# One layer of a hybrid encoder on one core: the input projection as 7 block products, done whole before the branches

## The chip, the cores and the metric

The kernel runs on one core of a Trainium2 chip. The metric is the device time of one execution in microseconds, the median of several runs. The profiler also records one execution of its own.

## The reference, cut to what matters

544 token rows (512 of a new stream, 32 of a running one) of width 2048 go through one layer. All of it is float32.

```python
mod = jax.nn.silu(c) @ w_ada + b_ada                 # shift, scale, gate: one vector per stream
h = rmsnorm(x, norm_g) * (1.0 + scale) + shift       # 544 x 2048
z = h @ w_in                                         # 2048 x 15360, split into ten parts
ya = gmlp_mix(gelu(au), rmsnorm(gelu(av))) * silu(ag)            # gMLP branch, 1024 wide
yb = rglru(causal_conv(lx)) * silu(lg)                           # RG-LRU branch, 1024 wide
yc = rmsnorm(hgrn2_scan(silu(hq), hf, hi)) * silu(hg)            # HGRN2 branch, 8 heads of 128
ga, gb, gc = split(sigmoid(mg), 3)                               # mg: 3 x 2048 columns of z
out = (ga * (ya @ w_a) + gb * (yb @ w_b) + gc * (yc @ w_c)) @ w_out
y = rmsnorm(x + gate * out, final_g)
```

z has 120 column blocks of 128: 8 each for au, av, ag, lx, lg, hq, hf, hi, hg and 48 for mg.

## The kernel before, in words

Activations lie transposed: 128 features on the partitions, 544 tokens along the free axis, in two halves of 272 (`HF`). The products run in float32r, and every operand is split in two parts, `wh` (rounded) and `wl` (the rest), so that one float32 product becomes three matmuls: `wh`·high, `wh`·low, `wl`·high (line 213). A weight piece of 128 x 1024 is loaded by SyncE's queue into `raw` (line 1171), copied by ScalarE into `wh` (through the helper `act`, line 154) and subtracted by VectorE into `wl` (line 1189). This is `prepare`; it runs two items ahead (`AHEAD`), and `wh` and `wl` have three buffers each.

The work is a list of items, written in the order in which they run. An item is one weight piece: 8 row blocks x 3 matmuls x 2 halves = 48 matmuls of 272 columns. A column block of z (`z_block`) is two items, a block of a branch product (`p_block`) one, a block of the out product (`o_block`) two. For each item the loop issues loads, then the item's `pre`, then `prepare(i + 2)`, then its matmuls, then its `post`, which empties the accumulator `pm`; then `pump()` lets every running generator do one step up to its next `yield`. The generators hold the rest of the branches: `av_gen` and `gm_gen` (gMLP), `hg_gen` (13 steps for each HGRN2 head), `lru_gen`, `gate_gen` (the gate vector of `mod`, line 1043, on VectorE), `yc_gen`, `mix_gen`. Each engine takes its instructions in the order in which they were issued.

The order of the stages is: the start (64 items of `w_ss` for shift and scale, line 367; under them the first three column blocks of z, lines 402 to 421); gMLP; HGRN2, four column blocks of z to a head; the merge of branch 0 (for each of 16 output blocks a column block of mg, then a `p_block`); the merge of branch 2; RG-LRU; the merge of branch 1; the out product. So column blocks of z are spread over all stages but the last. Everything between the stages stays in on-chip memory (`arena_t`, 26 pieces of 552 columns).

Of the kernel before, what the change touches and what calls it, by code (L numbers as in the profile page):

```python
# [7 lines left out]
F32 = mybir.dt.float32  # L8
# [5 lines left out]
NP = 512  # L14
# [26 lines left out]
SLOT = T + 8  # L41
SMALL = 256


class Arena:


    def __init__(self, t, slots, smalls):
        self.t = t
        self.slots, self.smalls = slots, smalls  # L50
        self.busy = [False] * slots
        self.small_busy = [False] * smalls
        self.at = self.small_at = 0

    def get(self, n):
        if n <= SMALL:
            order = [(self.small_at + i) % self.smalls for i in range(self.smalls)]
            k = next((i for i in order if not self.small_busy[i]), None)
            if k is None:
                raise MemoryError("no small piece left")  # L60
            self.small_busy[k] = True
            self.small_at = (k + 1) % self.smalls
            o = self.slots * SLOT + k * SMALL
            return self.t[:, o:o + n], ("s", k, 1)
        m = -(-n // SLOT)
        if m == 1:
            order = [(self.at + i) % self.slots for i in range(self.slots)]
        else:
            order = range(self.slots - m, -1, -1)
        k = next((i for i in order if not any(self.busy[i:i + m])), None)  # L70
        if k is None:
            raise MemoryError(f"no {m} slots in a row: {self.busy}")
        for i in range(k, k + m):
            self.busy[i] = True
        if m == 1:
            self.at = (k + 1) % self.slots
        return self.t[:, k * SLOT:k * SLOT + n], ("b", k, m)

# [3 lines left out]
    def free(self, r):  # L82
        kind, k, m = r
        busy = self.small_busy if kind == "s" else self.busy
        for i in range(k, k + m):
            busy[i] = False


class Buf:
    def __init__(self, arena, n):  # L90
        self.arena, self.n = arena, n
        self.ap, self.r = arena.get(n)
        self.col = self.r[1] * SLOT

# [11 lines left out]
def hybrid_step_kernel(ctx: ExitStack, tc: tile.TileContext, xT, cT, w_first, w_in, w_branch, w_out,  # L106
# [4 lines left out]
    const = ctx.enter_context(tc.tile_pool(name="const", bufs=1))  # L111
    wp = ctx.enter_context(tc.tile_pool(name="wp", bufs=3))
    ps = ctx.enter_context(tc.tile_pool(name="ps", bufs=2, space=PSUM))

    h_a = const.tile([128, KW, 2, T], F32R, name="h_a")
    h_b = {}
    yH = const.tile([128, KW, 2, T], F32R, name="yH")
# [4 lines left out]
    masks = const.tile([128, len(LEVELS), 2, 128], U8, name="masks")  # L122
# [9 lines left out]
    cs = const.tile([128, KD, 2], F32, name="cs")  # L132
    outs_conv = const.tile([128, KW, 2, 3], F32, name="outs_conv")
    outs_h = const.tile([128, KW, 2], F32, name="outs_h")
    NSLOT, NSMALL = 26, 5
    arena_t = const.tile([128, NSLOT * SLOT + NSMALL * SMALL], F32, name="arena_t")
    arena = Arena(arena_t, NSLOT, NSMALL)

    def buf(n=T):
        return Buf(arena, n)  # L140
# [26 lines left out]
    def pm():  # L167
        return ps.tile([128, 2, 512], F32, tag="m", name="pm", bufs=2)
# [19 lines left out]
    def hT(k):  # L188
        return h_a[:, k] if k < KW else h_b["t"][:, k - KW]

    def yT_in(k):
        return yH[:, k]

    def split(dst, src):
        act(dst[:, 0, :], src, AF.Copy)
        tt(dst[:, 1, :], src, dst[:, 0, :].bitcast(F32), op=OP.subtract)


    items = []

    def item(src, width, mul, post=None, pre=None, plain=False):
        items.append((src, width, mul, post, pre, plain))

    def group_item(src, kt, rhs, acc, first, last, post, pre=None, hs=(0, 1)):
# [1094 lines left out]
```

## Time and profile before

| | us |
|---|---|
| median of 3 runs (2178.68 to 2179.18) | 2178.73 |
| the profiled execution, its own time | 2176.01 |
| its span, first to last instruction | 2174.3 |
| TensorE (PE) busy in the span | 2128.7 |
| VectorE (DVE) busy | 891.0 |
| ScalarE (ACT) busy | 761.2 |
| GpSimd (POOL) busy | 287.9 |

Matmuls are pipelined, so that the busy time of PE is the time in which at least one is under way; PEld is the load of the stationary operand. The span is what the rows below divide up; the time of an execution lies 1.7 us above it, and the median of the runs 2.7 us above that.

### The profile page before, as it was taken

The numbers are of one execution on the slowest core, as the hardware profiler recorded it, in microseconds if no ns is written. First come the engines' busy times: TensorE is split into PE (matmuls) and PEld (weight loads), VectorE is DVE, ScalarE is ACT, GpSimd is POOL, SyncE is SP. The second block draws the span as 40 slices with busy tenths as digits, with TensorE's granted clock in tenths as the row PEclk, the third lists the DMA queues.
The fourth block names the chain that finished last, engine by engine and source line by source line (L and its number), as shares of the span: only waits on it lengthen the run. The fifth ranks groups of instructions, "written<-read, shape, count | busy, mean of one in ns | idle before, by whom it ended". The sixth has DMA issues, their size and how long they took to land.

```text
span 2174.3 us, 39091 instructions
## 1 busy us (share of the span) xinstructions
PE 2128.7 (98%) x17048; PEld 2070.3 (95%) x17048; DVE 891.0 (41%) x1306; ACT 761.2 (35%) x1116; POOL 287.9 (13%) x308
## 2 busy tenths in 40 slices
PE   6989999999999999999999999999999999999997
PEld 3689999999999999999999999999999999999997
DVE  3432323344444444222223655525555352244225
ACT  3233433455455555322222222224655222233223
POOL 0000100212233333000000010011111001111112
PEclk9999999999999999999999999999999999999999
DMA  9942222222222222222222544422222442223334
GB/s 354 392 137 85 83 86 79 89 70 73 82 75 70 80 73 72 82 84 89 90 87 82 169 142 144 127 81 82 90 86 90 128 136 89 88 86 122 106 123 146
DMA packets 77355, 241.95 MB, mean 111 GB/s; under 512 B 8608, under 2 KB 15040, under 8 KB 77184
## 3 DMA queue, kind: packets, MB, share of 16 engines
q1 hardware_dynamic: 75184, 236.96, 33.4%
q8 instruction: 134, 2.20, 0.4%
q10 hardware_dynamic: 1376, 1.28, 0.2%
q0 software_dynamic: 624, 1.21, 0.2%
q14 instruction: 37, 0.30, 0.0%
HBM read 233.75 MB, written 5.67 MB: 110 GB/s over the span
## 4 chain that ended last, share of the span: by engine, by line
PE 94%; DMA 2%; DVE 1%; ACT 1%; issue 0%; SPq 0%; POOL 0%; DVEq 0%; ACTq 0%
PE pm L213 86%; DMA arena_t<-in_w_first_dram 1%; PE px L651 1%; PE pm L421 1%; ACT arena_t L154 1%; PE px L367 1%; PE po L304 0%; PE po L421 0%; PE px L730 0%; DMA raw<-in_w_in_dram 0%; PE px L511 0%; PE po L787 0%; PE px L770 0%; DMA arena_t<-in_xT_dram 0%; PE px L653 0%
## 5 line engine op out<-in xcount | busy, mean ns | idle before, releaser
L213 PE MATMUL pm<-h_b,wh 128*128 128x272 f32 x4256 | 714.4, 289 | 0.0
L213 PE MATMUL pm<-h_a,wh 128*128 128x272 f32 x4256 | 712.8, 289 | 0.1
L1189 DVE TENSOR_TENSOR wl<-raw,wh 128x1024 fp32r<-128x1024 f32 (+1 forms) x328 | 404.8, 1234 | 604.4 <-ACT wh L154 601.3
L213 PEld LDWEIGHTS pm<-h_a,wh 128*128 128x128 f32 x4256 | 603.1, 188 | 1.8 <-ACT wh L154 0.3
L213 PEld LDWEIGHTS pm<-h_b,wh 128*128 128x128 f32 x4256 | 601.4, 188 | 1.9 <-ACT wh L154 1.4
L154 ACT ACTIVATE wh<-raw 128x1024 fp32r<-128x1024 f32 (+1 forms) x328 | 339.1, 1037 | 522.7 <-PE pm L213 474.4
L213 PE MATMUL pm<-h_a,wl 128*128 128x272 f32 x2128 | 443.1, 288 | 0.8 <-DVE wl L1189 0.8
L213 PE MATMUL pm<-h_b,wl 128*128 128x272 f32 x2128 | 443.6, 288 | 0.0
L213 PEld LDWEIGHTS pm<-h_b,wl 128*128 128x128 f32 x2128 | 336.4, 188 | 0.0
L213 PEld LDWEIGHTS pm<-h_a,wl 128*128 128x128 f32 x2128 | 334.5, 188 | 1.0 <-DVE wl L1189 1.0
L213 PE MATMUL pm<-yH,wh 128*128 128x272 f32 x1536 | 255.5, 288 | 0.0
L154 ACT ACTIVATE arena_t<-pm 128x544 f32<-128x544 f32 (+3 forms) x143 | 80.2, 573 | 440.4 <-PE pm L213 431.6
L213 PEld LDWEIGHTS pm<-yH,wh 128*128 128x128 f32 x1536 | 217.4, 188 | 0.2
L1006 POOL TENSOR_TENSOR arena_t<-arena_t 128x544 f32<-128x544 f32 x32 | 61.0, 1906 | 793.4 <-DVE arena_t L1004 739.7
L213 PE MATMUL pm<-yH,wl 128*128 128x272 f32 x768 | 158.5, 288 | 0.0
L154 ACT ACTIVATE arena_t<-arena_t 128x272 f32<-128x272 f32 (+6 forms) x181 | 98.5, 583 | 160.0 <-DVE arena_t L1101 100.3
L213 PEld LDWEIGHTS pm<-yH,wl 128*128 128x128 f32 x768 | 120.2, 188 | 0.0
L1043 DVE SCALAR_TENSOR_TENSOR arena_t<-arena_t,cs 128x512 f32<-128x512 f32 x120 | 92.1, 826 | 10.2 <-DMA arena_t<-in_w_gate_dram 10.2
L1004 DVE TENSOR_TENSOR arena_t<-pm,arena_t 128x544 f32<-128x544 f32 x48 | 34.8, 725 | 146.7 <-PE pm L213 146.7
L154 ACT ACT_TABLE_LOAD x59 | 75.7, 1283 | 30.7 <-PE pm L213 25.2
L154 ACT ACTIVATE arena_t<-px 128x512 f32<-128x512 f32 (+3 forms) x96 | 34.6, 377 | 84.9 <-PE px L754 32.2
L154 ACT ACTIVATE yH<-arena_t 128x544 fp32r<-128x544 f32 (+1 forms) x40 | 27.2, 693 | 96.9 <-DVE arena_t L915 36.9
(218 smaller groups left out, 1220.2 us busy)
## 6 DMA issues: line engine op xcount, KB each, us to landing
raw<-in_w_in_dram SPq DMA_DIRECT2D x234, 512.0 KB, 3.7
raw<-in_w_ss_dram SPq DMA_DIRECT2D x54, 512.0 KB, 9.8
raw<-in_w_branch_dram SPq DMA_DIRECT2D x48, 512.0 KB, 3.5
raw<-in_w_out_dram SPq DMA_DIRECT2D x38, 512.0 KB, 3.8
arena_t<-in_w_gate_dram SPq DMA_DIRECT2D x64, 256.0 KB, 4.2
arena_t<-in_xT_dram SPq DMA_DIRECT2D x16, 544.0 KB, 6.7
arena_t<-in_w_ss_dram SPq DMA_DIRECT2D x10, 512.0 KB, 7.0
out_yT_dram<-arena_t SPq DMA_DIRECT2D x12, 272.0 KB, 2.6
```

Source lines behind the costliest of these rows:

```text
L154: return nc.scalar.activation(out, in_, func, **kw)
L213: mm(p[:, h, :HF], w[:, s], rhs(k)[:, r, h * HF:(h + 1) * HF], start=first and i == 0 and q == 0, stop=last and i == n - 1 and q == 2)
L367: mm(p[32 * i:32 * i + 32, part * 256:part * 256 + 256], cz[:, 4 * q + i, :], w[:, i * 256:(i + 1) * 256], start=q == 0, stop=q == 3)
L421: mm(firsts[g][:, h, :HF], w[:, s], hT(k)[:, r, h * HF:(h + 1) * HF], start=k == 0 and q == 0, stop=k == KD - 1 and q == 2)
L651: mm(fv(p, 64 * i, [[128, 2], [1, 64]]), x[:, 256 * i + 128:256 * i + 256], fv(x, 256 * i, [[256 + m, 2], [2 * m, nb], [1, m]]), start=Tru ...
L1004: tt(two(g.ap), halves(p), two(g.ap), op=OP.mult)
L1006: ptt(mix[j].ap, mix[j].ap, g.ap, op=OP.add)
L1043: stt(acc[s].ap, b.ap, c, acc[s].ap, op0=OP.mult, op1=OP.add)
L1189: tt(wl[:, :width], t[:, :width], wh[:, :width].bitcast(F32), op=OP.subtract)
```

## The change

h is cut into 2 x 2 blocks (two halves of the tokens, two halves of the 2048 features), and a pair of column blocks of z with its 2048 weight rows into 2 x 2 blocks as well. One level of Strassen's scheme (in Winograd's form) makes the four block products of the pair's outputs out of 7 products instead of 8: `group`. A product is an item of 8 x 3 = 24 matmuls of 272 columns. The seven sums of h (`X[1]` to `X[7]`) are formed once, in the start (`sums`); the weight sums are formed for every pair on VectorE, into the raw pieces and one buffer `t2`; VectorE adds up the outputs in `after`. There are 60 pairs, all done in one stretch directly after the start (`z_groups`). The three column blocks that ran under the start now run there too.

There isn't room on the chip for z, so blocks go to device memory: hf, hq, hi, hg and all of mg by `keep`, av after its gelu, and the finished branch outputs ya and yb. gMLP and RG-LRU run as generators under the pairs; the gates of RG-LRU are plain float32 matmuls now (4 for a block, before 12 in float32r). Then `merges` runs the three branches' products, 16 `p_block`s each, with no column blocks of z between them: branch 0 with HGRN2 heads 0 to 3, branch 1 with heads 4 to 7 and `gate_gen`, and branch 2 after the last head. A `p_block` lets the generators step three times (after 18, 36 and 48 matmuls). The gate blocks of mg, the partial sums `mix`, ya, yb and a head's four blocks are loaded from device memory on GpSimd's queue, which also takes the loads of `gate_gen` and, in the out product, of x.

```diff
+PRODUCTS = (1, 6, 2, 5, 7, 3, 4)
+RAWS = 6
+    def halved(src, width=1024):
+        wh = wp.tile([128, 1024], F32R, tag="wh", name="wh", bufs=3)
+        wl = wp.tile([128, 1024], F32R, tag="wl", name="wl", bufs=3)
+        split(wh[:, :width], wl[:, :width], src[:, :width])
+        return wh, wl
+    def rows3(p, w, rhs, kt, start, stop, **kw):
+        wh, wl = w
+        n = len(kt)
+        for i, k in enumerate(kt):
+            s = slice(i * 128, (i + 1) * 128)
+            for q, (a, r) in enumerate(((wh, 0), (wh, 1), (wl, 0))):
+                mm(p, a[:, s], rhs(k, r), start=start and i == 0 and q == 0,
+                   stop=stop and i == n - 1 and q == 2, **kw)
+    def group(b1, b2, post, posts=None):
...
+                if i == 1:
+                    g["w", 1] = halved(raws[n11])
+                elif i == 6:
+                    a, b, c = raws[n11], raws[n12], raws[n22]
+                    tt(a, b, a, op=OP.subtract)
+                    t = g["t"] = late["t2"]
+                    tt(t, c, a, op=OP.subtract)
+                    g["w", 6] = halved(t)
+                elif i == 2:
+                    g["w", 2] = halved(raws[n21])
+                elif i == 5:
+                    g["w", 5] = halved(raws[n11])
+                    done[n11] = True
+                elif i == 7:
+                    tt(raws[n12], raws[n22], raws[n12], op=OP.subtract)
+                    g["w", 7] = halved(raws[n12])
+                    done[n12] = True
+                elif i == 3:
+                    g["w", 3] = halved(raws[n22])
+                    done[n22] = True
+                elif i == 4:
+                    t = g["t"]
+                    tt(t, raws[n21], t, op=OP.subtract)
+                    g["w", 4] = halved(t)
+                    done[n21] = True
...
+        bank = {1: 0, 2: 0, 6: 1, 5: 2, 3: 2, 7: 3, 4: 3}
...
+                if i == 1:
+                    g["u"] = buf(HF)
+                    act(g["u"].ap, b, AF.Copy)
+                elif i == 6:
+                    tt(g["u"].ap, b, g["u"].ap, op=OP.add)
+                elif i == 2:
+                    g["o1"] = buf()
+                    act(g["o1"].ap[:, :HF], b, AF.Copy)
+                elif i == 5:
+                    g["o2"] = buf()
+                    tt(g["o2"].ap[:, HF:], b, g["u"].ap, op=OP.add)
+                elif i == 7:
+                    o = g["o2"].ap[:, HF:]
+                    tt(o, b, o, op=OP.add)
+                elif i == 3:
+                    tt(g["o2"].ap[:, :HF], b, g["u"].ap, op=OP.add)
+                elif i == 4:
+                    tt(g["o1"].ap[:, HF:], b, g["u"].ap, op=OP.add)
+                    g.pop("u").free()
+                    post(g.pop("o1"), g.pop("o2"))
...
+            for lo, hi in zip((0, *cuts), (*cuts, n)):
+                for h in hs:
+                    rows3(p[:, h, :HF], [a[:, lo * 128:hi * 128] for a in w], lambda k, r: rhs(k, r, h), kt[lo:hi],
+                          first and lo == 0, last and hi == n, skip_group_check=True)
+                if hi < n:
+                    pump()
...
+                   lambda k, r, h: X[pair[h]][:, k, r, :], p, True, True, lambda: post(p), pre, cuts=(3, 6))
...
+    def sums(c):
+        x = st["x"][c]
+        lo, hi = x[:, :, :HF], x[:, :, HF:]
+        if c < 4:
+            put(1, c, lo)
+            tt(st["s3"], lo, hi, op=OP.subtract)
+            put(7, c, st["s3"])
+            return
+        y = st["x"][c - 4]
+        a11, a21 = y[:, :, :HF], y[:, :, HF:]
+        tt(a21, a21, hi, op=OP.add)
+        tt(a11, a21, a11, op=OP.subtract)
+        put(6, c, a11)
+        put(2, c, lo)
+        put(5, c, a21)
+        tt(lo, lo, a11, op=OP.subtract)
+        put(3, c, lo)
+        put(4, c, hi)
...
-                            if c > 1 and n < 3:
-                                first_mul(c - 2, 1, n)
-                            if n > 4:
-                                first_mul(c - 1, 0, n - 5)
...
+        u, sg = cell["o"]
...
+        act(u.ap, u.ap, AF.Gelu_apprx_tanh)
+        act(t1.ap, sg.ap, AF.Sigmoid)
+        tt(sg.ap, sg.ap, t1.ap, op=OP.mult)
+        tt(sg.ap, sg.ap, u.ap, op=OP.mult)
...
+    def hg_gen(h):
+        if h == 0:
+            hg_setup()
+        cell = {}
+        zf, zq, zi, zg = (hbuf() for _ in range(4))
+        for b, n in ((zf, "hf"), (zq, "hq"), (zi, "hi"), (zg, "hg")):
+            nc.gpsimd.dma_start(out=b.ap, in_=scratch[f"{n} {h}"])
+        yield
...
+        act(t1.ap, zf.ap, AF.Abs)
+        ts(g.ap, zf.ap, 0.0, None, op0=OP.min)
+        act(t2.ap, zf.ap, AF.Relu)
...
+        act(zf.ap, zq.ap, AF.Sigmoid)
+        nc.gpsimd.memset(qb.ap[:, 0:1], 0.0)
+        tt(qb.ap[:, 1:], zq.ap, zf.ap, op=OP.mult)
+        act(zf.ap, zg.ap, AF.Sigmoid)
+        stt(zg.ap, zg.ap, P("onorm_g"), zf.ap, op0=OP.mult, op1=OP.mult)
...
+    def lru_gen(b, x, sg):
+        xs, w = buf(NS + 3), buf(256)
+        nc.gpsimd.dma_start(out=w.ap, in_=lru_w[b].rearrange("p a n -> p (a n)"))
...
+        act(x.ap, sg.ap, AF.Sigmoid)
+        tt(sg.ap, sg.ap, x.ap, op=OP.mult)
+        x.free()
+        yield
+        yield
...
+                mm(ri[n][h], w.ap[:, n * 128:(n + 1) * 128], xc.ap[:, h * HF:(h + 1) * HF], start=True, stop=True)
+        w.free()
+        yield
...
+        light = [(B_HF + h, B_HQ + h, keep(f"hf {h}", f"hq {h}")) for h in range(8)]
+        light += [(B_HI + h, B_HG + h, keep(f"hi {h}", f"hg {h}")) for h in range(8)]
+        light += [(B_MG + j, B_MG + j + 1, keep(f"mg {j}", f"mg {j + 1}")) for j in range(0, 48, 2)]
...
+        for i in range(40):
+            if i % 5 in (0, 2):
+                b1, b2, post, at_start = heavy[i // 5 * 2 + (i % 5) // 2]
+                group(b1, b2, post, {1: at_start} if at_start else None)
...
+        def pre(j):
+            def f():
+                if j == 0:
+                    fetch(0)
+                fetch(j + 1)
+                act(got["g", j].ap, got["g", j].ap, AF.Sigmoid)
+                if on:
+                    on(j)
+            return f
...
-                    nc.sync.dma_start(out=b.ap, in_=w_gate[n, :, k + i, :])
+                    nc.gpsimd.dma_start(out=b.ap, in_=w_gate[n, :, k + i, :])
...
+        def on0(j):
+            if j == 0:
+                open_hgrn()
+                start(y_gen(1, (2, 5)))
+            if j % 4 == 0:
+                start(hg_gen(j // 4))
+        def on1(j):
+            if j % 4 == 0:
+                start(hg_gen(4 + j // 4))
+            if j == 0:
+                start(yc_gen())
+            if j == 4:
+                start(gate_gen())
+        def on2(j):
+            if j == 0:
+                while "yc" not in ready:
+                    pump()
+        merge(0, (1, 6), on0)
+        merge(1, (2, 5), on1)
+        merge(2, (1, 6), on2)
```

## Rows read from the trace of the kernel before

**Rows 1.** The page's totals: engine, busy us (share of the span) xinstructions.
```profile
PE 2128.7 (98%) x17048; PEld 2070.3 (95%) x17048; DVE 891.0 (41%) x1306; ACT 761.2 (35%) x1116; POOL 287.9 (13%) x308
```

**Rows 2.** The chain of work that ended last, share of the span by engine.
```profile
PE 94%; DMA 2%; DVE 1%; ACT 1%; issue 0%; SPq 0%; POOL 0%; DVEq 0%; ACTq 0%
```

**Rows 3.** Stretches of the span: engines' busy us (instructions), granted clock, DMA share, GB/s.
```profile
54.00:108.00 54.00, 53.12 (x520) 35.39 (x523) 23.53 (x61) 15.24 (x28) 0.00 (x0) 1.00 1.01 395
122.00:135.00 13.00, 13.00 (x86) 13.00 (x86) 4.78 (x10) 5.97 (x9) 1.09 (x1) 0.80 0.36 127
600.00:800.00 200.00, 200.00 (x1604) 191.29 (x1604) 92.47 (x166) 106.84 (x203) 62.66 (x72) 1.00 0.24 73
1000.00:1200.00 200.00, 200.00 (x1595) 200.00 (x1594) 52.77 (x51) 45.01 (x52) 0.00 (x0) 1.00 0.29 89
```

**Rows 4.** Groups by line and shape, whole span: count | busy us, mean ns | idle before.
```profile
L213 PE MATMUL pm<-h_a,wh 128*128 128x272 f32 x4256 | 712.8, 289 | 0.1
L213 PE MATMUL pm<-h_b,wl 128*128 128x272 f32 x2128 | 443.6, 288 | 0.0
...
L1043 DVE SCALAR_TENSOR_TENSOR arena_t<-arena_t,cs 128x512 f32<-128x512 f32 x120 | 92.1, 826 | 10.2 <-DMA arena_t<-in_w_gate_dram 10.2
L154 ACT ACT_TABLE_LOAD x59 | 75.7, 1283 | 30.7 <-PE pm L213 25.2 <-issue 2.8 <-PEq L1279 1.7
L1004 DVE TENSOR_TENSOR arena_t<-pm,arena_t 128x544 f32<-128x544 f32 x48 | 34.8, 725 | 146.7 <-PE pm L213 146.7
```

**Rows 5.** Groups by line from 1000 to 1200 us: the weight preparation.
```profile
L1189 DVE TENSOR_TENSOR wl<-raw,wh 128x1024 fp32r<-128x1024 f32 x33 | 40.4, 1225 | 109.0 <-ACT wh L154 107.8
...
L154 ACT ACTIVATE wh<-raw 128x1024 fp32r<-128x1024 f32 x33 | 34.9, 1058 | 96.5 <-PE pm L213 96.5
```

**Rows 6.** Timeline of the out product's last, single-half blocks: start, length, instruction, count.
```profile
2127.58 0.41 PE L213 MATMUL pm<-h_a,wh 128*128 128x272 f32 x2
...
2130.57 0.41 PE L213 MATMUL pm<-h_b,wh 128*128 128x272 f32 x2
```

**Rows 7.** Timeline from the last product of the start to the first z item.
```profile
111.73 0.64 PE L367 MATMUL px<-raw,arena_t 128*32 128x256 f32 x8
...
121.18 3.07 PE L421 MATMUL pm<-h_b,yH 128*128 128x272 f32 x12
...
128.48 1.67 PE L421 MATMUL pm<-h_b,yH 128*128 128x272 f32 x12
...
130.75 0.67 PE L213 MATMUL pm<-h_a,wh 128*128 128x272 f32 x4
```

**Rows 8.** Timeline of one RG-LRU block on VectorE: what ended the idle time stands in brackets.
```profile
1510.05 2.33 DVE L915 SCALAR_TENSOR_TENSOR arena_t<-arena_t,par 128x512 f32<-128x512 f32 x3
...
1527.58 0.72 DVE L944 SCALAR_TENSOR_TENSOR arena_t<-arena_t 128x544 f32<-128x544 f32 x1 [3.67 <-ACT arena_t L154]
...
1530.38 1.22 DVE L949 TENSOR_TENSOR_SCAN arena_t<-arena_t 128x512 f32<-128x512 f32 x1
```

**Rows 9.** Timeline of one HGRN2 head: its first ScalarE, VectorE and GpSimd steps.
```profile
592.87 0.62 ACT L154 ACTIVATE arena_t<-pm 128x544 f32<-128x544 f32 x1 [4.40 <-PE pm L213]
...
601.76 1.34 POOL L595 TENSOR_TENSOR arena_t<-arena_t 128x544 f32<-128x544 f32 x1 [2.12 <-ACT arena_t L154]
...
607.37 1.27 DVE L600 TENSOR_TENSOR_SCAN arena_t<-arena_t 128x544 f32<-128x544 f32 x1
...
608.67 0.45 ACT L154 ACTIVATE arena_t<-arena_t 128x288 f32<-128x288 f32 x1 [2.88 <-DVE arena_t L600]
```

**Rows 10.** Who waited for whom, 395 to 880 us: us in total, times, longest.
```profile
PEld px L651 <- ACT arena_t L154: 1.0, 1, 1.0
```

**Rows 11.** DMA issues: count, KB each, median us from issue to landing.
```profile
out_yT_dram<-arena_t SPq DMA_DIRECT2D x12, 272.0 KB, 2.6
```

**Rows 12.** Groups by line from 390 to 860 us, VectorE and GpSimd.
```profile
L1189 DVE TENSOR_TENSOR wl<-raw,wh 128x1024 fp32r<-128x1024 f32 x62 | 80.7, 1301 | 97.1 <-ACT wh L154 97.1
...
L814 POOL DMA_DIRECT2D out_S_new_dram<-arena_t x7 | 4.1, 591 | 0.0
```

More of the change, by code (lines that the diff above doesn't have):

```diff
@@ L82, in free @@
     def free(self, r):
[L83 to L86, printed above, removed]
+        for i in range(r[0], r[0] + r[1]):
+            assert self.busy[i]
+            self.busy[i] = False
 class Buf:
@@ L186, in newton @@
         stt(y, t, 1.5, y, op0=OP.add, op1=OP.mult)
[L188 to L204, printed above, removed]
-        def mul(wh, wl):
-            p = acc()
-            n = len(kt)
-            for i, k in enumerate(kt):
-                s = slice(i * 128, (i + 1) * 128)
-                for q, (w, r) in enumerate(((wh, 0), (wh, 1), (wl, 0))):
-                    for h in hs:
-                        mm(p[:, h, :HF], w[:, s], rhs(k)[:, r, h * HF:(h + 1) * HF],
-                           start=first and i == 0 and q == 0,
-                           stop=last and i == n - 1 and q == 2)
-        item(src, len(kt) * 128, mul, post, pre)
@@ new lines, in split_rows, with spill, need, item @@
+    def split_rows(pair, k, src):
+        for h in range(2):
+            x = X[pair[h]]
+            split(x[:, k, 0, :], x[:, k, 1, :], src[:, h * HF:(h + 1) * HF])
+    scratch = {}
+    def spill(name, n=T, rows=128):
+        scratch[name] = tc.dram_tile([rows, n], F32, name="d_" + name.replace(" ", "_"))
+        return scratch[name]
+    items, loads = [], []
+    done, raws = {}, {}
+    def need(src, width=1024):
+        loads.append((src, width))
+        return len(loads) - 1
+    def item(prep, mul, post=None, pre=None):
+        items.append((prep, mul, post, pre, len(loads)))
@@ new lines, in hybrid_step_kernel, with load_some @@
+    at = {"load": 0}
+    EARLY = 34
+    def load_some(upto):
+        while at["load"] < min(upto, len(loads)):
+            n = at["load"]
+            e = "early" in pools.open_ and n < EARLY and n % 5 < 2
+            back = [i for i in raws_order["early" if e else "raw"]]
+            if len(back) >= (3 if e else RAWS) and not done.get(back[-(3 if e else RAWS)]):
+                return
+            src, width = loads[n]
+            if e:
+                t = early["p"].tile([128, 1024], F32, tag="raw0", name="raw0", bufs=3)
+            else:
+                t = wp.tile([128, 1024], F32, tag="raw", name="raw", bufs=RAWS)
+            raws_order["early" if e else "raw"].append(n)
+            nc.sync.dma_start(out=t[:, :width], in_=src)
+            raws[n] = t
+            at["load"] += 1
```

867 lines of the change are left out of this document (400 added, 467 removed).

## The prediction

> **What bounds the kernel now.** I read the totals and the chain first: PE is busy in 98% of the span and holds 94% of the chain [rows 1, 2]. The stretches then tell whether that is work or only being busy: from 1000 to 1200 us PE runs 1595 matmuls in 200 us, one in 125.4 ns, and in the HGRN2 stage (600 to 800 us) 1604, while VectorE is busy for 52.8 and 92.5 us of 200 [rows 3]. So after the start the time is the number of matmuls times their pace. The groups give the number: line 213 has 4256 matmuls with `h_a,wh` and 2128 with `h_b,wl`; each of the two has a twin on the other half, so 12768 in z and out, of which 11232 are z (117 blocks x 96) [rows 4]. What feeds PE waits for PE: of 200 us, VectorE stood 107.8 before its `wl` subtractions waiting for ScalarE's `wh`, and `wh` 96.5 for PE to release a buffer [rows 5]. That is the slack which the change spends. In the HGRN2 stage PE waited for a generator hardly at all: the listed wait of `px` loads on ScalarE is 1.0 us in all [rows 10]; a step of a head had a whole item, 48 matmuls or 6.0 us, to be done in.
>
> **The change part by part.** The sum is made on the span of 2174.3.
>
> *Matmuls.* 60 pairs x 7 products x 24 = 10080 instead of 11232 after the start. The three blocks under the start cost nothing there, where the DMA is full at 395 GB/s [rows 3], and now cost like the rest, so the scheme's 1440 saved are only 1152: -144.5 us. The new order puts 24 matmuls in a row into one bank, where two alternate now. The out product's last blocks do just that: 24 matmuls from 2127.58 to 2130.57, 124.6 ns each [rows 6]; the pace stays. RG-LRU's gates go from 96 fast matmuls (12 us) to 32 plain float32 ones; no row has their price; between 125 ns each as a fast one (4 us) and twice the 256 ns of a matmul at the low clock [rows 7] (16 us) I take 15, so +3. Together -141.5.
>
> *Start.* 3.1 MB less to load at 395 GB/s takes 8 us off the last `w_ss` product (111.73, [rows 7]): about 104. Behind it come `h_make(7)` and `sums(7)`, some 3 + 5 VectorE operations of 0.72 that alternate with ScalarE's copies, about 15 us in all, and the preparation of product 6 (two sums, `wh`, `wl`: 2 x 1.23 + 1.06 + 1.23 = 4.7), under part of which product 1 runs. The even stream of products thus begins as if at 122.6 instead of 130.75: -8 (0 to -15).
>
> *Pairs.* A pair takes PE 168 x 125.4 ns = 21.1 us. VectorE has 4 weight sums and 7 `wl` of 1.225 [rows 5] and 5 output sums of half 0.725 plus the fixed part, 0.44 [rows 4]: 15.7. ScalarE has 7 x 1.06 and two copies: 8.3. Both fit, and the order fits: product 6 is the tightest, from the release of a buffer 0.44 + 2.45 + 1.06 + 1.23 = 5.2 us, of 6.0 that two products last. So light pairs run at PE's pace. The weights are 2 MB in 21 us, 100 GB/s, and two spilled blocks 27 more, of 395 that were moved: no bound.
> With 0.8 us in hand, every extra piece in VectorE's queue shows. An RG-LRU generator puts its convolution (3 x 0.75 and five small ones, 4.0 [rows 8]) behind the output sum of product 4, then a sum that waits for a sigmoid. `wl` of product 2 comes 2.5 us late, of which the gates' matmuls use 1.8. Two steps later tanh, a table load of 1.28 [rows 4], exp and square stand before a VectorE operation; the row before shows that it waited 3.67 us for them [rows 8]. Behind it are the weight sum and `wl` of product 4, and the output sum that must empty its bank: 3.7 late. Then come both scans (1.48) ahead of the next pair's two sums: 2.9 late. In all 7.5 net, x 8 = 60. A gMLP group puts gelu, a table load, sigmoid and four VectorE operations (2.4) there: 1.75 late x 8 = 14. Transposes of av and the setups: 12. Together +86 (40 if the queue regains half of it, 140 if each generator step costs a whole one).
>
> *Merge of branches 0 and 1.* 32 `p_block`s with 8 heads under them. A head now has a `p_block` of 6.0 us for three of its steps, before one item for each. Take 0 as the end of a `p_block`'s matmuls before a new head. VectorE's product of 0.73, then on GpSimd a spill, the loads of the next gate block, and `hf`, 0.59 each to issue [rows 12], and 2.6 to land [rows 11]: hf is there at 5.1. The first step took from 592.87 to 603.10 before [rows 9], 10.2 us: 15.3. The scan follows two operations that wait for two sigmoids, at about 16, and ScalarE's copy of its result ends 1.75 after the scan's start (607.37 to 609.12, [rows 9]): 17.7. Next in ScalarE's queue are the gate's sigmoid (0.62) and the next `wh` (1.06), then the copy that the head's first matmul reads: 20.1. PE until then has 18 + 12 + 18 + 18 matmuls and the former head's transposes: 9.1. It stands for about 10. The later steps lose 3 more (levels, states and outputs each wait 1 to 2 us for ScalarE or VectorE with 1.5 to 2.3 us of matmuls as cover). 13 x 8 = +104 (5 a head if half of the first step lies ahead, 20 if GpSimd's loads queue up). After such a gap the clock falls: after 6 us of idling, 12 matmuls took 3.07 us at 121.18 and 1.67 at 128.48, with 0.80 granted in between [rows 3, 7]. Part of what this costs lies in later waits: +1.5 a head, 12. First item (ya splits late, masks loaded, yb split): +14. `mix` on GpSimd in branch 1: +8.
> `gate_gen` comes in at item 4 of branch 1: 120 operations of 0.826 = 99 us [rows 4], about 36 of its 42 steps under 12 `p_block`s, 7.5 us each. Before, they lay in stages where VectorE idled. Besides, VectorE has there 1.23 + 0.73 and a head's part: 92.5 less 33 x 1.225 for four heads in 200 us [rows 3], 13 a head, 3.3 an item; in sum 12.8 an item against 9 on PE with the head's matmuls. The excess alone is 45; added to the head's waits in full it would be 90. I take +48.
> Branch 2 waits for head 7, whose last two steps, with `gate_gen`'s between, and the split of its output run with PE idle: +18 (8 to 25). Branch 2 and the out product have the same matmuls as before: +1.
>
> A rule speaks against the merged order too. The Trainium skill, "SBUF — State Buffer", section "Who interferes with whom", has a VectorE instruction with two SBUF inputs contend with a GpSimd instruction that reads SBUF. The trace agrees: `wl` took 1225 ns on average where GpSimd was idle and 1301 in the HGRN2 stage [rows 5, 12]; at 1301 for all 660 sums and `wl` of the pairs, VectorE would have 50 us more to do, and a pair 16.5 us of 21.1, so the sum stands by either.
>
> *Sum:* 2174.3 - 141.5 - 8 = 2024.8, what it would be with PE never waiting. + 86 + 104 + 12 + 14 + 8 + 48 + 18 + 1 = 2315.8. An execution lies 1.7 above its span and the median shown 2.7 above that: 2320.
>
> **The rivals.**
> *The feeding engines keep ahead in the merges* (other side). If a head's first step ran under the matmuls of the `p_block` before, its 104 and 12 would fall away, and with VectorE's queue packed `gate_gen`'s 48: 2320 - 164 = 2156. It decides as soon as merges and the wait for head 7 lose under 63 us instead of 205. For it: all engines but PE were under half busy [rows 1]. Against it: hf is asked for only behind the product of the block before, in GpSimd's queue; and VectorE's demand in branch 1 is above PE's.
> *Heads one after the other, and worse.* Spills, loads, `mix` and a head's arithmetic share GpSimd's queue; if a head loses 20 and `gate_gen` 90, and the pairs 140: + 56 + 42 + 54 = 2472.
> *The scheme saves nothing.* If VectorE's 15.7 a pair were its pace with every generator added (60 x 15.7 + 8 x 9 for RG-LRU + 8 x 3.8 = 1044 us of 1264), there would be no loss by quantity; so this needs a slower pace of PE itself: 4% would give +51 on z, 2371. Rows 6 speak against it.
>
> **How the numbers follow.** The forecast, losses in pairs and merges above the gain, has 0.70; the first rival 0.17, the second 0.08, the third 0.02; 0.03 is left for losses that just cancel. A measurement of this kernel can't tell less than 0.2% (4 us) from no change. Faster 0.18, same 0.03, slower 0.79. The range takes in the lower bounds of pairs, heads and `gate_gen` together with the start's (2320 - 46 - 64 - 42 = about 2160) and above the middle of forecast and second rival: 2150 to 2410. The forecast's own range is 2230 to 2400.
>
> **What the changed profile would show.** Line of the products: 10080 matmuls of 272 columns at 125 ns in light pairs, no gap. In pairs with RG-LRU, PE loads waiting for VectorE's `wl` three times, 3 us each. In branches 0 and 1, every fourth `p_block`, PE waiting about 10 us for ScalarE before the head's first 128-wide matmuls, and a granted clock below 1; in branch 1 VectorE over 80% busy. A gap of 15 us before branch 2. The prediction is wrong if PE stays near 98% busy through the merges, or if light pairs already take more than 21.1 us.

## The result and the profile after

2700.3 us is the median of 4 runs (2696.1 to 2705.0), against 2178.7 for the kernel before: 1.2395 times as long, 95% interval 1.2373 to 1.2417. 2320 us were forecast, 2150 to 2410 as the range. The sign was right, the size was 380 us short.

The page's totals and its chain by engine; they answer to [rows 1] and [rows 2]:

```profile
PE 2118.7 (78%) x15608; PEld 1981.3 (73%) x15608; DVE 1527.2 (57%) x2063; ACT 1022.0 (38%) x1519; POOL 479.8 (18%) x714
...
PE 50%; DVE 21%; ACT 13%; issue 8%; DMA 4%; POOL 3%; ACTq 0%; DVEq 0%; SPq 0%; POOLq 0%
```

The 1440 matmuls fewer are there, but PE's share of the chain fell from 94% to 50%. Five stretches (columns as in [rows 3]): the start, light pairs (pairs whose outputs are only stored, nearly alone here), pairs with RG-LRU, a head of branch 0, and one of branch 1 with the gate:

```profile
54.00:108.00 54.00, 39.29 (x352) 15.14 (x352) 22.69 (x49) 22.79 (x41) 0.00 (x0) 0.66 0.90 334
300.00:400.00 100.00, 87.48 (x661) 83.47 (x660) 61.37 (x68) 35.23 (x40) 8.76 (x15) 1.00 0.34 109
1100.00:1300.00 200.00, 164.09 (x1181) 156.84 (x1180) 121.44 (x142) 72.11 (x87) 13.56 (x30) 0.96 0.28 92
1867.00:1926.00 59.00, 38.91 (x295) 35.77 (x295) 26.32 (x52) 31.85 (x60) 24.53 (x32) 0.86 0.29 97
2185.00:2274.00 89.00, 45.71 (x298) 41.60 (x298) 53.80 (x95) 31.19 (x60) 44.41 (x58) 0.69 0.37 130
```

A light pair should take 21.1 us; 661 matmuls in 100 us make 168 x 100 / 661 = 25.4, at a clock of 1.00. So in z, PE stands still at full clock. Where, the timeline of PE shows (only rows with a wait ahead, which stands in brackets):

```profile
525.19 0.49 PE L286 MATMUL pm<-x,wh 128*128 128x272 f32 x2 [0.63 <-DVE arena L349]
529.11 0.49 PE L286 MATMUL pm<-x,wh 128*128 128x272 f32 x2 [0.67 <-DVE arena L352]
532.97 0.49 PE L286 MATMUL pm<-x,wh 128*128 128x272 f32 x2 [0.63 <-DVE arena L354]
541.94 0.52 PE L286 MATMUL pm<-x,wh 128*128 128x272 f32 x2 [1.30 <-ACT arena L187]
546.31 0.52 PE L286 MATMUL pm<-x,wh 128*128 128x272 f32 x2 [1.09 <-DVE arena L343]
```

At five of seven boundaries PE waits until the bank of the product that it has just finished is emptied (L349 is the output sum of product 5, and the product that waits is 7; for product 1 it is ScalarE's copy), although the next product writes another bank: 4.3 us a pair, 60 x 4.3 = 258. The waits of PE over the whole span (us in total, times, longest) have the same names, and the heads' wait on top:

```profile
PE px L777 <- ACT harena L187: 170.2, 8, 31.6
PE pm L286 <- ACT arena L187: 86.9, 56, 10.8
PE pm L286 <- DVE arena L352: 61.7, 60, 3.2
PE pm L286 <- DVE arena L349: 49.9, 60, 2.1
PE pm L286 <- DVE arena L354: 39.5, 60, 2.6
PE pm L286 <- DVE arena L343: 32.3, 52, 1.1
```

The last output sum of z starts at 1800.6, and VectorE's last multiplication of a block by its gate in branch 1 at 2365.3. So z ends about 290 us late (the terms give 122.6 + 1264 + 15 + 86 = 1488, and its transposes and small products, which lie in the base, some 20), and the two branches take 565 us where 32 items of 9 with a head and the 186 of the other terms (104 + 12 + 14 + 8 + 48) make 474. 290 and 91 are the whole miss.

### The profile page after: what moved, and what is told of

The parts are those of the page before. It is cut to its first block, busy times and chain, and to the rows that moved or that the text cites. A ratio compares the mean times of both kernels' runs of the same rounds, so it can differ in the third digit from the quotient of the medians.

```text
span 2700.4 us, 38265 instructions
## 1 busy us (share of the span) xinstructions
PE 2118.7 (78%) x15608; PEld 1981.3 (73%) x15608; DVE 1527.2 (57%) x2063; ACT 1022.0 (38%) x1519; POOL 479.8 (18%) x714
## 3 DMA queue, kind: packets, MB, share of 16 engines
q0 software_dynamic: 30800, 101.12, 11.1%
## 4 chain that ended last, share of the span: by engine, by line
PE 50%; DVE 21%; ACT 13%; issue 8%; DMA 4%; POOL 3%; ACTq 0%; DVEq 0%; SPq 0%; POOLq 0%
PE pm L286 45%; ACT wh L187 5%; DVE wl L223 4%; ACT arena L187 3%; DVE t L322 2%; ACT harena L187 2%; DVE arena L1193 2%; DVE t L306 1%; DVE raw L304 1%; ACT L187 1%; DMA harena<-d_hf 1%; DVE arena L352 1%; ACT L191 1%; DVE arena L349 1%; DVE arena L343 1%
## 5 line engine op out<-in xcount | busy, mean ns | idle before, releaser
L286 PE MATMUL pm<-x,wh 128*128 128x272 f32 x8768 | 1755.6, 299 | 277.6 <-ACT arena L187 86.9
L286 PEld LDWEIGHTS pm<-x,wh 128*128 128x128 f32 x8768 | 1423.1, 195 | 340.4 <-issue 181.7
L286 PE MATMUL pm<-x,wl 128*128 128x272 f32 x4384 | 1291.2, 295 | 1.0 <-DVE wl L223 1.0
L286 PEld LDWEIGHTS pm<-x,wl 128*128 128x128 f32 x4384 | 853.1, 195 | 1.2 <-DVE wl L223 1.2
L223 DVE TENSOR_TENSOR wl<-raw,wh 128x1024 fp32r<-128x1024 f32 x386 | 482.5, 1252 | 348.8 <-ACT wh L187 348.5
L187 ACT ACTIVATE wh<-raw 128x1024 fp32r<-128x1024 f32 x386 | 405.6, 1051 | 337.1 <-DVE raw L314 250.1
L187 ACT ACTIVATE wh<-t 128x1024 fp32r<-128x1024 f32 x120 | 127.2, 1060 | 558.4 <-DVE t L306 365.6
L223 DVE TENSOR_TENSOR wl<-t,wh 128x1024 fp32r<-128x1024 f32 x120 | 147.1, 1226 | 144.5 <-ACT wh L187 144.5
L777 PE MATMUL px<-harena 128*128 128x128 f32 x160 | 37.4, 372 | 199.1 <-ACT harena L187 170.2
L777 PEld LDWEIGHTS px<-harena 128*128 128x128 f32 x160 | 30.0, 262 | 203.2 <-ACT harena L187 174.5
L187 ACT ACTIVATE arena<-arena 128x544 f32<-128x544 f32 (+3 forms) x150 | 82.1, 550 | 87.0 <-DVE arena L1260 62.6
L1193 DVE SCALAR_TENSOR_TENSOR arena<-arena,cs 128x512 f32<-128x512 f32 x120 | 101.5, 907 | 21.2 <-DMA arena<-in_w_gate_dram 21.0
L306 DVE TENSOR_TENSOR t<-raw 128x1024 f32<-128x1024 f32 x60 | 73.5, 1226 | 2.0
```

Source lines behind the costliest of these rows:

```text
L187: return nc.scalar.activation(out, in_, func, **kw)
L223: tt(lo, src, hi.bitcast(F32), op=OP.subtract)
L286: mm(p, a[:, s], rhs(k, r), start=start and i == 0 and q == 0, stop=stop and i == n - 1 and q == 2, **kw)
L306: tt(t, c, a, op=OP.subtract)
L777: mm(fv(p, 64 * i, [[128, 2], [1, 64]]), x[:, 256 * i + 128:256 * i + 256], fv(x, 256 * i, [[256 + m, 2], [2 * m, nb], [1, m]]), start=Tru ...
L1193: stt(acc[s].ap, b.ap, c, acc[s].ap, op0=OP.mult, op1=OP.add)
```

## The experiments

Times are medians of 4 runs; the kernel before stood at 2175.5 to 2178.0 beside them. "z ends" is the start of its last output sum, "two branches" the time from there to the start of VectorE's last multiplication by the gate in branch 1. e7 leaves out the heads and the gate vector, so its time is not that of a whole layer.

| kernel | us | z ends | two branches |
|---|---|---|---|
| as changed | 2700.3 | 1800.6 | 564.7 |
| e1_four_tiles | 2447.1 | 1547.3 | 562.6 |
| e2_bank_order | 2500.1 | 1605.1 | 560.7 |
| e3_gate_in_z | 2653.8 | 1846.1 | 493.6 |
| e4_head_loads | 2652.8 | 1797.7 | 520.6 |
| e5_memset | 2439.3 | 1536.7 | 567.0 |
| v1_combined | 2389.8 | 1616.3 | 461.3 |
| v2_lead1 / v2_lead2 | 2394.9 / 2391.0 | 1618.2 / 1618.9 | 464.0 / 457.7 |
| v3_sigmoid_z | 2366.9 | 1618.4 | 438.2 |
| v3_gate_wide | 2378.3 | 1605.5 | 458.8 |
| v4_all / v4_lead2 | 2348.3 / 2344.8 | 1604.2 / 1596.3 | 438.4 / 433.7 |
| v5_gate_fine | 2391.8 | 1620.5 | 461.2 |
| v5_all_fine | 2339.4 | 1595.2 | 434.6 |
| e7_no_heads | 2052.3 | 1544.8 | 195.0 |
| v6_sums_early | 2377.7 | 1480.6 | 559.2 |
| v6_lead2 / v6_all_fine | 2262.8 / 2245.8 | 1512.9 / 1501.4 | 435.0 / 432.7 |

**Is it the shared tile?** Banks 0 and 1 are one PSUM tile, 2 and 3 another. The first experiment gives each bank a tile, the second only exchanges banks.

```
-    pms = [ps.tile([128, 2, 512], F32, ...) for i in range(2)]
-    banks = [pms[i // 2][:, i % 2, :HF] for i in range(4)]
+    zp = pools.open("zp", "left", space=PSUM)
+    banks = [zp.tile([128, 512], F32, name=f"pz{i}")[:, :HF] for i in range(4)]
...
-    bank = {1: 0, 2: 0, 6: 1, 5: 2, 3: 2, 7: 3, 4: 3}
+    bank = {1: 0, 2: 0, 6: 2, 5: 1, 3: 1, 7: 3, 4: 3}
```

> Four PSUM tiles of one bank each for the products of z; two tiles of two banks only once the merges begin. Theory (a product waits for the output sum of the product before it because two banks are one tile, so an output sum has to be through before the next product starts): a light pair falls from 25.4 us to 21.1 to 21.6, that is 60 x 4 = 240 us, and some of the further 155 us that z lost under generators comes back: 2370 to 2450 us against 2700. Rival (VectorE's and ScalarE's work for a pair sets its pace, by amount or by order of preparation): a light pair stays at 25 us, 2670 to 2700.

> Still two tiles of two banks, but the banks of products 6 and of 5 and 3 are exchanged, so that only one boundary of a pair (2 to 5) has two products in a row in one tile, instead of five. Theory of the shared tile: a light pair at 21.1 + 0.9 = 22 us, four fifths of the gain of four tiles: 2420 to 2500 us. Rival (VectorE's and ScalarE's work sets the pace): 2670 to 2700.

z ends 253.3 us sooner with four tiles and 195.5 with the banks exchanged: the one boundary that is left costs 57.8, 0.96 us in each of 60 pairs. The branches stay as they were. The shared tile is shown as the cause of these 253 us, by removal and by its amount; the second time lies at the edge of what was expected. The stretch of light pairs with four tiles:

```profile
500.00:600.00 100.00, 98.88 (x786) 98.49 (x785) 73.26 (x82) 39.91 (x46) 8.42 (x15) 1.00 0.39 130
```

786 matmuls in 100 us, 21.4 us a pair. The Trainium skill, "Perfetto Trace Analysis", section "Matmuls", has independent groups rotate through different banks, so that emptying one overlaps the next. These banks did rotate; the overlap came only when the tiles did too.

**The gate and the heads' loads.** The gate leaves branch 1 for the last pairs of z; and a head's four loads are issued one `p_block` ahead (`hg_load`).

```
-            if j == 4:
-                start(gate_gen())
...
+            if i == 29:
+                group(*light[i], posts={2: lambda: start(slow(gate_gen(), 2))})
...
+            if j % 4 == 3:
+                hg_load(j // 4 + 1)
```

> The gate's 120 VectorE operations leave branch 1 and are spread over the last ten pairs of z, a step every second product. Theory (gate_gen and the heads together overload VectorE's queue in branch 1): the four heads there fall from 64 to 91 us each to about 58, as in branch 0, so branch 1 takes 323 - 92 = 230 us; in z each of 42 steps of about 2.4 us on VectorE stands ahead of an output sum that a product waits for, +50 to +100. Together 2610 to 2710 us. Rival (branch 1 is slower for its mix on GpSimd and the splits of finished heads): branch 1 stays above 300 us, 2750 to 2800 in all.

> The four loads of a head are issued one p_block earlier (under the block before its start) for seven of eight heads. Theory (the first step starts late because its loads stand in GpSimd's queue behind the product of the block before, and take 6.3 us to land): ScalarE's wait of 8.3 us before Abs goes, each of seven heads is 5 to 8 us shorter: 35 to 55 us off, 2645 to 2665. Rival (the head's first matmuls wait for ScalarE's queue, in which the gate's sigmoid and the weight copies stand, whenever the loads land): within 10 us of 2700.

Both times fell where expected. Without the gate, branch 1 takes 250.9 instead of 323.3 us from the end of branch 0 (72 less, where 92 were expected), and from its last multiplication to branch 2's first there are 10.5 instead of 27.4 us: 89 us off, 45 given back in z. What the gate cost in branch 1 is not only VectorE's work. VectorE's waits as changed, from 2042 to 2366 us, show its queue standing 25.3 us for the gate's own weights, which GpSimd's queue had asked for late:

```profile
DVE arena L1193 <- DMA arena<-in_w_gate_dram: 15.0, 7, 7.6
DVE arena L1191 <- DMA arena<-in_w_gate_dram: 10.3, 2, 9.6
```

No run separates this part from the rest.

The loads: a block ends on PE at 1866.5, and VectorE's multiplication starts at 1867.91, behind operations of the former head. The timeline of GpSimd in the kernel as changed then has the load of hf fifth:

```profile
1869.16 0.54 POOL L1143 DMA_DIRECT2D d_mix<-arena  x1 [13.53 <-ACT arena L187]
1869.69 0.54 POOL L940 DMA_DIRECT2D out_S_new_dram<-harena  x1
1870.23 0.54 POOL L941 DMA_DIRECT2D out_S_new_dram<-harena  x1
1870.76 0.54 POOL L1119 DMA_DIRECT2D arena<-d_mg  x1
1871.29 0.54 POOL L688 DMA_DIRECT2D harena<-d_hf  x1
```

ScalarE's timeline there: its first operation on hf, and the copy of the scan's result:

```profile
1877.60 1.20 ACT L187 ACTIVATE harena<-harena 128x544 f32<-128x544 f32 x2 [8.34 <-DMA harena<-d_hf]
...
1891.64 0.44 ACT L187 ACTIVATE harena<-harena 128x288 f32<-128x288 f32 x1 [2.69 <-DVE harena L726]
```

PE's timeline: the block's last matmul, this head's first matmuls (it is the second of branch 0) and later ones, and the first of the fourth head:

```profile
1866.20 0.29 PE L286 MATMUL pm<-x,wl 128*128 128x272 f32 x1
...
1894.70 1.22 PE L777 MATMUL px<-harena 128*128 128x128 f32 x4 [17.32 <-ACT harena L187]
...
1903.63 0.61 PE L777 MATMUL px<-harena 128*128 128x128 f32 x4
...
2010.11 1.22 PE L777 MATMUL px<-harena 128*128 128x128 f32 x4 [15.95 <-ACT harena L187]
```

With the loads ahead, the timeline of PE in the same two heads:

```profile
1886.91 1.22 PE L781 MATMUL px<-harena 128*128 128x128 f32 x4 [14.31 <-ACT harena L187]
...
1993.00 1.22 PE L781 MATMUL px<-harena 128*128 128x128 f32 x4 [6.82 <-ACT harena L187]
```

The wait falls by 3.0 us in the second head and by 9.1 in the fourth; over the two branches the gain is 44 us, some 6 for each of seven heads. In the fourth, part of it comes back: a later group of L781 waits 3.4 us for ScalarE where that of L777 waited 0.4 for VectorE.

**The start.** The `w_ss` products use z banks in turn, and the next memset stands ahead of the sums in VectorE's queue.

```
-                            st["ada"] = px()
-                            nc.vector.memset(st["ada"], 0.0)
+                            st["ada"] = zt[2 + c % 2]
...
+                        if n == 1 and c < 7:
+                            nc.vector.memset(zt[2 + (c + 1) % 2], 0.0)
```

> On top of four tiles: the w_ss products write two of the four z banks in turn, and the memset of the next one stands in VectorE's queue ahead of the sums of the block before instead of behind them. Theory (each block of the start takes 13 us instead of 10.6 because PE waits 3.5 to 4.5 us for that memset): the last w_ss product falls from 117 to about 104 us, and the whole by 8 to 13: 2434 to 2439 us against 2447. Rival (the loads, or the chain of shift, h and sums itself, set those 13 us): within 3 us of 2447.

7.8 us off four tiles, as expected. The last `w_ss` product is not at 104 but at about 111, and the DMA rate of the start is 364 GB/s, not the 395 of [rows 3]: so the memset was about half of those 13 us, not all.

**All three, and longer cover for the heads.**

> Four tiles, the gate under the last ten pairs of z, and a head's loads one p_block ahead, together. If the three causes are separate, the gains add: 2447 less 89 for the gate (72 in branch 1, 17 before branch 2), less 47 for the loads, plus what the gate costs in z, 10 to 45 (less than the 45 of two tiles, since an output sum behind the gate's operations no longer holds up the next product): 2320 to 2356 us. If they are one and the same loss seen three times, it stays above 2380.

> As the combined version, but each head but the first starts one p_block earlier, with three more turns: one behind its loads, one behind its first step, one ahead of its first matmuls; its inputs lie in the other arena. Theory (what is left of a head's loss is the latency of the chain Abs to sigmoid to scan to copy, 17 us against 9 us of matmuls, and PE's in-order queue): with 7 us more of cover a head falls from 53 to 40 us, 7 x 13 = 90 us off: 2230 to 2270. Rival (two heads at once overload ScalarE's queue, with a table load of 1.28 us at each change of function): within 25 us of the combined version.

> As the version with a lead of one p_block, with a lead of two and six turns more. If latency still sets the heads, a further 10 to 30 us off; if the amount of work of VectorE or ScalarE per head does (some 30 us a head), no change within 10 us; if the overlap of two heads costs ScalarE further table loads, slower.

The first missed: by its time it is on the side of "one and the same loss". By its parts it is not: the branches fell by 101 us of the 115 that both gains make (71 and 44), but the gate now cost z 69 us, more than the 45 with two tiles; why it does is not shown. The lead theory fell: 2394.9 and 2391.0 against 2389.8. PE's wait ahead of a head's first matmuls did shrink with the lead of two (39.8 us over the branches, 9 times, with 93.8 in 11 without a lead), and 62.4 us came up in its place before the head's output matmuls, for VectorE's copies of the states (L925). The waits of PE with a lead of two, from 1600 to 2080 us:

```profile
PE po L939 <- DVE harena L925: 62.4, 7, 9.6
PE px L795 <- ACT harena L193: 39.8, 9, 18.8
```

**ScalarE's queue, and the gate spread out.**

> As the combined version, but the sigmoid of the branch gates is taken in z, ahead of their spill, and not in each p_block. Theory (what sets a head now is ScalarE's queue, busy 34 us of 54, in which each p_block's sigmoid brings a table load of 1.28 us before it and one behind it): up to 4 x (0.66 + 2 x 1.28) = 13 us a head go from that queue, a head falls from 54 to 42 to 48 us, 8 x 6 to 12 us off, z gains 0 to 15: 2295 to 2355 us against 2390. Rival (the hand-over between the engines of a head's chain, whatever else stands in ScalarE's queue): within 20 us of 2390.

> As the combined version, with the gate's 42 steps spread over 30 pairs of z and not 15 to 18. Theory (the gate cost 69 us in z because VectorE's work there, 15 x 15.7 for the pairs, 32 for RG-LRU and 82 for the gate, 350 us, was above PE's 317): over 30 pairs it has 30 x 15.7 + 60 + 99 = 630 us of 633, so the amount just fits and 69 falls to 20 to 40: 2340 to 2361 us. Rival (each step of the gate costs its time wherever it stands): 2385 to 2395.

> Four tiles, the earlier memset, the gate over 30 pairs, a head's loads ahead and the sigmoid in z, all together. If the gains are separate: 2390 - 8 - 40 - 70 = about 2270 us (2230 to 2310), still slower than the kernel before, whose 2178 would need the 32 p_blocks and eight heads of branches 0 and 1 in some 250 us, where PE alone has 264 at the full clock.

> As the version with everything together, but heads with a lead of two p_blocks and six more turns. If ScalarE's queue was what made the lead useless before, the lead now pays: 15 to 50 us below the version with everything together. If the heads are bound by the amount of work of ScalarE and VectorE, within 10 us of it.

None is as its theory had it. The sigmoid gives 23 us, not 35 to 95: ScalarE's queue is part of a head's length, not all that sets it. The gate over 30 pairs still costs z 58 us. All together take 2348, outside the 2230 to 2310; the gains as measured do add (2389.8 less 22.9, 11.5 and 7.8 is 2347.6), so it is the gains expected that were too large. The lead gives 3.5 us more, within a measurement.

**What leaves VectorE no room in z?**

```
-            if i == 9:
-                group(*light[i], posts={2: lambda: start(slow(gate_gen(), 4))})
+            if i == 2:
+                group(*light[i], posts={2: lambda: start(slow(gate_gen(), 1))})
...
                             stt(acc[s].ap, b.ap, c, acc[s].ap, op0=OP.mult, op1=OP.add)
+                        yield
```

> As the version with the gate over 30 pairs, but a step is one operation of 0.83 us instead of up to four, one every second product. Theory (what the gate costs in z is the length of a step: up to 3.3 us at once in VectorE's in-order queue, where a product has 3.0 us and VectorE 0.8 us of that to spare): its 58 us in z fall to 10 to 25, 2330 to 2345 us against 2378. Rival (the amount of VectorE's work): within 10 us of 2378.

> As the version with everything together and a lead of two p_blocks (2345 us), with the gate in steps of one operation, and the steps of RG-LRU and gMLP cut in two to five, one or two VectorE operations in each. By the length of a step: 40 us off for the gate and 20 to 40 for RG-LRU and gMLP, 2265 to 2300. By the amount of work: 2335 to 2350.

With single operations the gate costs z 73 us, more than before. That does not clear the length of a step, for the edit changed two more things. The gate starts seven light pairs sooner (its operations stand from 352 to 945 us, before from 555 to 1141), one behind each product and not every second one as expected. And its weights are asked for one product before their use and not four, so VectorE's queue now stands for them; its waits from 340 to 960 us have

```profile
DVE arena L1210 <- DMA arena<-in_w_gate_dram: 27.6, 10, 5.7
```

where the version with 30 pairs has no such wait. Cut steps in RG-LRU and gMLP, together with this gate, leave z where it was (1595.2 against 1596.3); since the finer gate alone made z 15 us longer, they may have given that much, but no run has them alone. The timeline of VectorE with four tiles shows why 15.7 us of operations nearly fill a pair:

```profile
509.72 1.22 DVE L310 TENSOR_TENSOR raw<-raw 128x1024 f32<-128x1024 f32 x1
510.97 1.22 DVE L312 TENSOR_TENSOR t<-raw 128x1024 f32<-128x1024 f32 x1
513.40 1.23 DVE L229 TENSOR_TENSOR wl<-t,wh 128x1024 fp32r<-128x1024 f32 x1 [1.21 <-ACT wh L187]
514.54 0.43 DVE L362 TENSOR_TENSOR arena<-pz,arena 128x272 f32<-128x272 f32 x1
514.90 1.22 DVE L229 TENSOR_TENSOR wl<-raw,wh 128x1024 fp32r<-128x1024 f32 x1
```

A sum, then 1.21 us in which VectorE can only wait for ScalarE to make `wh` of it, then `wl`; everything else of VectorE's stands behind. That comes three times a pair, 3.6 us; with the other waits for `wh` it is 4.2 (19.5 us listed from 500 to 600 us). The last three kernels issue each sum one product earlier; here the sum for product 7, and those for 6 and 4 likewise:

```
                 elif i == 5:
                     g["w", 5] = halved(raws[n11])
                     done[n11] = True
+                    tt(raws[n12], raws[n22], raws[n12], op=OP.subtract)
                 elif i == 7:
-                    tt(raws[n12], raws[n22], raws[n12], op=OP.subtract)
                     g["w", 7] = halved(raws[n12])
```

> Four tiles, and each weight sum is issued behind the wl of the product before, not directly ahead of its own wh and wl. Theory (VectorE stands 4.3 us a pair waiting for ScalarE's wh of the block it has just summed, so a pair takes 20.0 us of VectorE's queue and not 15.7, and anything a generator adds shows): the wait of wl for wh falls to under 1 us a pair, and of the 126 us that z still loses under generators 40 to 80 come back: 2365 to 2405 us against 2447. Rival (latency of each generator's step, whatever VectorE has in hand): within 15 us of 2447.

> As the version with everything together and a lead of two p_blocks (2345 us), with the sums one product earlier. By the theory the gate's 50 to 70 us in z fall to 0 to 15 as well: 2240 to 2290. By the rival: 2330 to 2345.

> The same with the gate in steps of one operation and RG-LRU and gMLP in short steps. If, with VectorE's time in hand, the length of a step now decides, 10 to 30 us below the version with long steps; if not, within 8 us of it.

All three times are as expected: 69, 82 and a further 17 us off. Light pairs run at PE's pace now, 795 matmuls in 100 us, 21.1 us a pair:

```profile
500.00:600.00 100.00, 99.95 (x795) 99.57 (x794) 73.71 (x83) 39.95 (x45) 7.68 (x15) 1.00 0.40 130
```

One sign did not come: VectorE's listed wait of `wl` for `wh` is 406.0 us over the span, 400.1 with four tiles. From 500 to 600 us it is 24.7 us, and PE has no listed wait there, so it holds nothing up. So the place of the sum is shown as the cause; whether the time in hand or the shorter way from a free buffer to `wl` (a sum less in it) does it, these runs do not tell apart. The gate in z did not become nearly free either: with the sigmoids it cost z 60 us before (1596.3 less the 1536.7 of e5) and costs some 43 now (1512.9 less 1480.6, with e5's 10.6 added, which is an estimate). The finer steps give 17 us once the sums are moved, as their expectation had it. So the length of a step may count after all; the gate's earlier start came with it, and this gate too waits for its weights (19.2 us).

**The branches without heads.**

> Four tiles, and the eight HGRN2 heads and the gate left out (branch 2 multiplies what the operands hold, S_new and the gate get constants): what branches 0 and 1 take without them. Theory (the heads and the gate are the whole excess of the merges): 32 x 6.0 and some 26 for the first item, about 218 us in place of 562, and some 17 less ahead of branch 2: 2444 - 344 - 17 = 2083 us. Rival (p_blocks with sigmoid, spill and mix are themselves above PE's pace): branches 0 and 1 above 250 us, 2115 or more.

195.0 us for 32 blocks, even less than expected, and PE busy all the time (one stretch, columns as above):

```profile
1545.00:1740.00 195.00, 194.66 (x1540) 194.69 (x1541) 67.65 (x81) 57.07 (x80) 69.05 (x104) 0.99 0.65 216
```

`mix`, spills and the first item cost next to nothing; 368 us of the branches are the heads and the gate, their own matmuls included.

The best version takes 2245.8 us, 1.0318 times the kernel before (1.0303 to 1.0334), so no version here beats it. Its branches take 433 us against 195. PE is busy in 332 of these (columns as above):

```profile
1501.00:1934.00 433.00, 332.43 (x2355) 302.95 (x2355) 242.80 (x443) 205.41 (x443) 226.81 (x298) 0.86 0.37 124
```

So it stands still for 101 us, some 13 a head; the rest above 195 is the heads' own matmuls, at a lower mean clock. Starting the heads one or two blocks ahead moved their wait rather than removed it; what would set them free stays open.

## Why the prediction was wrong, step by step

**The step that failed** is "Both fit, and the order fits", from which "So light pairs run at PE's pace" was drawn. Its quantities hold: matmuls at 125.8 ns, `wl` at 1226 to 1252 ns, sums at 0.43. But it put at nothing the wait of a product for the emptying of the one before. "The output sum that must empty its bank" stood in the working, for RG-LRU alone, and there for the same bank. With two banks in a tile a product waited for the sum of the product before it: 253 us of the 290 by which z was late, gone with four tiles.

What is left of z's lateness then is 39 us (1547.3 against 1488 and some 20). 12 of these are the start's, and 18 are pairs at 21.4 us for 21.1, if each of the 60 loses that. So the +86 for the generators was nearly right, some 9 short. The same step also added VectorE's operations to 15.7 us of 21.1, where in the order of its queue they take 19.9, since `wl` waits for `wh` of the sum just ahead; moving the sums gave 67 us of z once the tiles were apart, and brings z's end to 1480.6, below the forecast of it.

**Matmuls**: right, 24 in a row into one bank run at the old pace.

**Start**: wrong by 12 us. Product 1 came at 123.4, but product 6 at 137.9 and not 125.6, behind a wait of 9.4. What stands between the last `w_ss` product and product 6 took 20 us from that product's end, as forecast (15 + 4.7); the loss lies before, for the last `w_ss` product came at 117.2 and not at 104. That the memset of `px` stands behind the sums in VectorE's queue was not read from the code; it is about half of that (e5). PE's timeline of the kernel as changed:

```profile
91.42 0.61 PE L527 MATMUL px<-raw,cs 128*2 128x256 f32 x8 [0.68 <-DMA raw<-in_w_ss_dram]
95.57 1.03 PE L527 MATMUL px<-raw,cs 128*2 128x256 f32 x8 [3.53 <-DVE px L523]
108.60 1.03 PE L527 MATMUL px<-raw,cs 128*2 128x256 f32 x8 [4.47 <-DVE px L523]
...
117.21 0.63 PE L527 MATMUL px<-raw,cs 128*2 128x256 f32 x8 [0.54 <-DMA raw<-in_w_ss_dram]
...
137.91 0.82 PE L286 MATMUL pm<-x,wh 128*128 128x272 f32 x2 [9.44 <-ACT arena L187]
```

**Heads**: the mechanism was right, the size short. PE's first wait was to be about 10 us and was 17.3 in the head shown. hf was expected 5.1 us behind the block's last matmul and came after 11.1: VectorE's multiplication of the block began 1.4 late behind the former head's operations, two S_new stores of that head stood ahead of hf on GpSimd and weren't counted, and the load took 6.3 us to land, not the 2.6 of a store [rows 11]. The first step with its way through ScalarE took 17.1 us, not 15.0. A head of branch 0 takes 58 us instead of some 50 (4 x 9 + 13 + 1.5): some 60 of the 91 us that the branches lost beyond the forecast.

**The gate**: 72 us in branch 1 and 17 before branch 2, against 48 and a part of 18; the 24 more in branch 1 are most of the rest of the 91. The working had it as VectorE's amount of work, over 80% busy; in the stretch shown VectorE was busy 60% of the time, and in branch 1 its queue stood 25.3 us for the gate's weights, a wait that was put at nothing.

**Clock**: right in kind (0.86 in a head of branch 0, 0.69 in branch 1).

**The rivals**: none held as a whole. The first needed the branches to lose under 63 us; without heads and gate they do lose nothing. The second had the branches nearly right, and with its reason, GpSimd's shared queue, in part: 20 us a head (measured: 58 less 36 and less the 1.5 for the clock) and 90 for the gate (72, and 17 before branch 2). Its 140 in the pairs was for the generators, which is not what cost there. The third looked for slower pairs, but in PE's own pace, which kept. The losses of z had no rival of their own; a rival "two banks wait as one" would have had to be priced at 60 x 5 x 0.85 us.

## What to carry to other kernels

Before counting on overlap between banks, buffers or halves, look at what the waits are tied to: here the rows named the last user of the whole tile, not of the bank. Compare an engine's operations with the time that its queue takes in program order, including the waits inside it; with four tiles VectorE had 5.4 us a pair in hand by the one and 1.2 by the other. And where a stage lost its cover, price every transfer on the queue ahead of the one that matters, and a load by a load's own time. A load that comes too late also holds up what stands behind its user in that engine's queue, as the gate's weights did on VectorE for 25.3 us.

## What the runs showed of the hardware

Idle times of PE went with a lower granted clock in the start and in the branches, but not in the light pairs. In the light pairs PE stood still for 4.3 of 25.4 us, in pieces of up to 1.3 us, and the clock was 1.00 (the rows from 300 to 400 and from 525 us). In the start, before, it was 1.00 with PE busy 53 of 54 us [rows 3]; after, with PE busy 39 of 54 and waits of 3.5 us and more among the rest, it was 0.66, and eight `w_ss` matmuls behind a memset took 1.03 us (rows above) where others took 0.61. Behind the wait of 17.3 us a head's first four matmuls took 1.22 us, and four of the same shape 9 us later 0.61 (rows above). In the two branches the mean clock was 0.77, without heads 0.99; the stretch of both branches as changed:

```profile
1801.00:2366.00 565.00, 339.46 (x2380) 310.21 (x2378) 311.11 (x562) 262.58 (x503) 258.78 (x350) 0.77 0.34 118
```

What the lower clock costs in all, no run here shows.
